# Holding side work behind later instructions in the attention stages of a hybrid decoder step

## The chip, the cores and the metric

The kernel runs on one core of one Trainium2 chip. A core has a matrix engine (TensorE, PE in the profile, with its weight loads as PEld), a vector engine (VectorE, DVE), an activation engine (ScalarE, ACT), a general engine (GpSimd, POOL) and a queue engine (SyncE, SP) that issues most of the transfers. The metric is the device time of one execution in microseconds (us); lower is better. Each engine works through its own list of instructions, whose order is fixed when the kernel is built.

## The reference, cut to what matters

One inference step of a one-layer decoder trunk is computed, for a prompt of 512 tokens and for a sample group of eight sequences of eight new tokens, each with 2048 tokens in a paged cache. Two attention branches run beside each other: forgetting attention ("fox") and sparse attention ("nsa"), which has a compressed, a selected ("slc") and a window ("win") part. Prompt and sample share all weights. Cut to what the change touches:

```python
def fox_attend(q, cq, q_pos, k, v, ck, k_pos):
    s = jnp.einsum('btgrd,bsgd->bgrts', q, k).astype(jnp.float32) * HEAD_DIM ** -0.5
    bias = jnp.moveaxis(cq, 1, -1)[..., :, None] - jnp.moveaxis(ck, 1, -1)[..., None, :]
    p = masked_softmax(s + bias, k_pos[None, :] <= q_pos[:, None])
    return jnp.einsum('bgrts,bsgd->btgrd', p.astype(v.dtype), v)

# in nsa_attend: which 16 of the blocks of 64 keys a query reads
imp = block_importance(jnp.sum(p_c, axis=2), n_sel)          # from the compressed scores
score = jnp.where(blk <= cur, imp + jnp.where(forced, FORCE_BONUS, 0.0), -jnp.inf)
_, idx = lax.top_k(score, min(N_SELECT, n_sel))
```

## The kernel before, in words

The change touches two stages.

**Prompt attention** (about 290 to 443 us of the trace). Its loop `for n, (br, r) in enumerate(steps + [(None, None)])` takes twelve steps: slc0, slc1, win0, win1, slc2, slc3, win2, win3, fox0 to fox3. A step scores two heads (g = 0, 1) in four query tiles each: two or three matmuls into one of four PSUM banks ("mm"), one vector instruction that adds the bias, writes the scores to SBUF and leaves their extreme (`tensor_tensor_reduce`, line 1253; `Swin`, `Sfox` in the profile; its instruction is kept as `last_min`), and one exponential on ACT (kept as `last_soft`). In the same step the step before is finished: its weights are turned over on PE (`ptwin`, `ptfox`), copied to SBUF by ACT and, one in three, by DVE (`turn_over`; `PTwin`, `PTfox`), multiplied with the values into a bank of a second pair ("acc"; `owin`, `ofox`), and scaled on DVE (`Wwin`, `oT`). Between these lie pieces of the conditioning projection (`adat`, `ada`, `adw`, `modT`).

Three steps also build the queries of later steps: `qstack` is called at n = 2 (nsa, second half), n = 6 (fox, first half, read from fox0 on) and n = 8 (fox, second half). It turns four tiles over into an "acc" bank for each of two heads, and for each of two halves of that bank ACT writes the rounded queries (line 1216) and DVE the rest (`stt`, line 1217, an instruction by `scalar_tensor_tensor` at line 110; `qstnsa`, `qstfox`). So one stack is four `stt` on DVE, each after an ACT instruction, and the ACT instruction of a bank's second half after the `stt` of its first.

The sample group's selection of blocks is computed beside this, as side work: `sample_cmp` at n = 2 (softmax of the compressed scores), `sample_importance` at n = 3, `sample_compare` at n = 6 (three pairwise comparisons of 30 x 30), `sample_rank` at n = 7 (two sums over them, lines 1446 and 1447, and four small ones), `sample_select` at n = 8 (tables and the turned selection). Most of it is DVE work; it writes tiles of a scratch that the profile calls `Dt`, and `rank`.

**Sample attention** (from 443 us). The loop over s = 0 to 15 takes a pair of sequences n = s // 4 and a quarter i = s % 4 of their cache: `key_rows` turns key rows over (`k`) and copies them (`kt`, by ACT and by DVE), `pair_scores` scores (`ss`) and takes the extreme on DVE (line 1794, `sS`) and the exponential on ACT, `turn_weights` turns over (`sp`, copied to `spT`), `values` multiplies (`so`). Rows come from HBM through the SP queue, a few quarters ahead. Beside it, `forget_split` cuts a sequence's sums of log forget values in three bf16 parts (`DH`, with `DR` as scratch: two ACT and two DVE instructions), for the sequences 0 and 1 ahead of the loop and for later pairs in the steps s = 1, 5, 9. `sample_maps` builds the tables that sort the summed rows (`maps`: one GpSimd instruction and fifteen DVE ones), ahead of the loop; the first `sums`, after s = 4, read them.

**What sets the order.** The program lists its instructions in the order of writing; a planner then puts each engine's instructions in an order of its own, by when its inputs are ready in its plan and, among those that are ready, the one written first. `issue_after(x)` holds every instruction of its block that runs on the engine of x behind x, and does nothing to the other engines' ones. The side work is held behind `last_min`, the last `tensor_tensor_reduce` of its step.

Of the kernel before, what the change touches and what calls it, by code (L numbers as in the profile page):

```python
# [6 lines left out]
F32 = mybir.dt.float32  # L7
# [3 lines left out]
AF = mybir.ActivationFunctionType  # L11
OP = mybir.AluOpType
# [16 lines left out]
LOW = -3.0e38  # L29
# [17 lines left out]
class Step:  # L47
# [1002 lines left out]
    def prompt_attention(self, pk, pn, pp):  # L1050
# [22 lines left out]
        for n, (br, r) in enumerate(steps + [(None, None)]):  # L1073
# [64 lines left out]
            side = {2: self.sample_cmp, 3: self.sample_importance, 6: lambda: self.sample_compare(pn), 7: self.sample_rank,  # L1138
                    8: self.sample_select}
            if n in side:  # L1140
                with self.tc.issue_after(self.last_min):
                    side[n]()
            if n == 11:
                with self.tc.issue_after(self.last_min):
# [60 lines left out]
    def qstack(self, pp, which, c0, gi, rp, gs=(0, 1)):  # L1205

        st = {}
        for g in gs:
            tb = self.stackb(f"q{which}{rp}{g}")
            for i in range(4):  # L1210
                self.tr(tb[:, P * i:P * i + P], self.zc(c0 + 64 * (4 * g + 2 * rp), P)[:, i])
            for e in range(2):
                lo = slice(64 * e, 64 * e + 64)
                hi = slice(64 - 64 * e, 128 - 64 * e)
                s = pp.tile([P, SEQ], F32R, tag="qst", bufs=4, name=f"qst{which}{rp}{g}{e}")
                self.act(s[lo], tb[lo], scale=self.gcol[lo, gi:gi + 1])
                self.stt(s[hi], tb[lo], self.gcol[lo, gi:gi + 1], s[lo].bitcast(F32), OP.mult, OP.subtract)
                st[g, e] = s
        return st

# [409 lines left out]
    def sample_attention(self, sp, sp0):  # L1630
        nc = self.nc
        self.E = self.op2.tile([P, 4, 64], BF16, name="E")
        self.tt(self.E, self.tok[:, 0:4, None].to_broadcast([P, 4, 64]), self.hot[:, None, :].to_broadcast([P, 4, 64]), OP.mult)
        self.chain = ""
        self.wk, self.S, self.DT, self.T, self.stat = {}, {}, {}, {}, {}
        self.sob = [self.accb(f"so{x}") for x in range(2)]
        self.keys, self.DH = {}, {}
        self.rooms(sp)
        for o in range(2):
            self.key_rows(sp, 0, o)  # L1640
            self.forget_split(sp, o)
            self.forget_turned(sp, o)
        for b in range(2):
            self.window_load(sp, b)
        for u in range(6, 11):
            self.sample_load(sp, u)
        self.sample_maps(sp)
        ns = 2 * NB
        for s in range(ns + 1):
            n, i, on = s // 4, s % 4, s < ns  # L1650
            if on:
                if i == 2:
                    for o in range(2):
                        self.window_keys(sp, 2 * n + o)
                self.pair_scores(sp, s)
                if i == 2:
                    self.window_scores(sp, n)
                    self.window_weights(n)
                if i == 1:
                    for o in range(2):  # L1660
                        if n < 3:
                            self.forget_split(sp, 2 * n + 2 + o)
            if s + 1 < ns:
                self.key_rows(sp, s + 1, 0)
            if on and i == 3:
                self.window_turned(sp, n)
            for g in range(2):
                if s:
                    self.values(s - 1, g)
            if s and i == 0:  # L1670
                self.pair_end(sp, n - 1)
            if s + 1 < ns:
                self.key_rows(sp, s + 1, 1)
            if i == 3 and n < 3:
                for o in range(2):
                    self.forget_turned(sp, 2 * n + 2 + o)
            if s == ns - 4:

                self.hH = self.keep.tile([P, NK, NT], F32R, tag="r2", bufs=1, name="hH")
                late = self.small.tile([P, 1], F32, tag="late", bufs=1, name="late")  # L1680
                with self.tc.issue_after(nc.gpsimd.tensor_copy(late, self.keys[0, 0][:, 0:1]).ins):
                    self.dma("gpsimd", self.hH, self.hfd[:, :, 0:NT])
            if on:
                for g in range(2):
                    self.turn_weights(sp, s, g)
            if s == ns:
                self.g0 = self.mix_first(self.w0, self.mmb, 0)
            if s == ns or n and i == 1:
                self.sums(n - 1)
            if on and i == 3:  # L1690
                self.window_values(sp, n)
                self.window_end(sp, n)
                for o in range(2):
                    if n < 3:
                        self.window_load(sp, 2 * n + 2 + o)
            for u in (2 * s + 9, 2 * s + 10):
                if s and u < 4 * NB:
                    self.sample_load(sp, u)
            if s == ns - 2:

                sp0.close()
                self.mix_open()
# [67 lines left out]
    def pair_scores(self, sp, s):  # L1770

        n, i = s // 4, s % 4
        bs = 2 * n, 2 * n + 1
        bd = self.bdF, self.bdN
        pbs = [self.mmb(f"ss{s}{g}") for g in range(2)]
# [14 lines left out]
        nm, dn = self.stat[n]  # L1790
        S = self.S[s] = [sp.tile([P, 576], F32, tag=f"S{2 * (s % 2) + g}", bufs=1, name=f"sS{s}{g}") for g in range(2)]
        ttr, w = self.nc.vector.tensor_tensor_reduce, 512
        for g in range(2):
            ttr(S[g][:, 0:512], pbs[g], self.ramp[g], -1.0, -LOW, OP.add, OP.min, nm[:, i, g:g + 1])
        if i == 3:
            w = 576
            pn = self.mmb(f"sn{n}")
# [7 lines left out]
                    own[:, g:g + 1])  # L1805
            self.tt(nm[:, 3], nm[:, 3], own, OP.min)
        for g in range(2):
            self.act(S[g][:, 0:w], S[g][:, 0:w], AF.Exp, bias=nm[:, i, g:g + 1], scale=-1.0, accum_out=dn[:, i, g:g + 1])

    def turn_weights(self, sp, s, g):  # L1810
        S = self.S[s][g]
# [883 lines left out]
```

## Time and profile before

| | us |
|---|---|
| median of 3 runs (1158.37 to 1158.73) | 1158.49 |
| the profiled execution's own time | 1155.07 |
| its span | 1153.4 |
| PE busy | 1131.6 (98% of the span) |
| DVE busy | 801.5 (69%) |
| ACT busy | 581.0 (50%) |
| POOL busy | 275.7 (24%) |

Times inside the trace are counted in us from the start of the span. The profiled execution ran 3.42 us under the median of the runs, and its span is 1.67 us shorter than its own time. Busy time says how long an engine had an instruction in work; matmuls overlap, so PE at 98% is not PE at its best rate. The granted clock of TensorE was 1.0 throughout.

### The profile page before, as it was taken

To read this page: it belongs to the slowest core of one execution; us is meant where nothing else is said; L and a number is where in the kernel's file an instruction comes from. 1 tells how busy PE (TensorE), PEld (TensorE's weight loads), DVE (VectorE), ACT (ScalarE), POOL (GpSimd) and SP (SyncE) were. 2 spreads that over 40 slices of the span, in tenths; PEclk is the share of its full clock that TensorE was granted. 3 is DMA by queue.
4 is the path that set the end of the run, shared out by engine and by line. 5 is a ranking of instruction groups with operands and counts; after the bars stand their busy time and mean duration, and the time that the engine had idled before them with its cause. 6 is when DMAs were issued, how large, how long until landed. Compare 5 with 4: busy or idle time off the path is not lost.

```text
span 1153.4 us, 25215 instructions
## 1 busy us (share of the span) xinstructions
PE 1131.6 (98%) x9434; PEld 966.6 (84%) x9434; DVE 801.5 (69%) x1937; ACT 581.0 (50%) x1151; POOL 275.7 (24%) x337
## 2 busy tenths in 40 slices
PE   8999999999999999999999999999999999999998
PEld 5888789999766565777899999789999998888887
DVE  4688785687776895776655454667867744798686
ACT  3455463444776785565532223447565655565420
POOL 4302100000220120001678670010656411110100
PEclk9999999999999999999999999999999999999999
DMA  9997456797684669999999994447444637877732
GB/s 221 229 263 222 151 152 200 242 319 237 191 257 160 209 213 317 293 317 328 233 287 301 330 289 159 119 132 223 148 149 147 188 113 255 318 257 252 240 119 83
DMA packets 188188, 255.51 MB, mean 222 GB/s; under 512 B 23161, under 2 KB 144706, under 8 KB 185890
## 3 DMA queue, kind: packets, MB, share of 16 engines
q1 hardware_dynamic: 148770, 173.03, 48.8%
q0 software_dynamic: 21296, 67.38, 18.2%
q10 hardware_dynamic: 18000, 13.50, 4.0%
q8 instruction: 74, 1.21, 0.4%
q14 instruction: 48, 0.39, 0.1%
HBM read 217.64 MB, written 57.12 MB: 238 GB/s over the span
## 4 chain that ended last, share of the span: by engine, by line
PE 82%; DVE 8%; issue 3%; DMA 3%; ACT 2%; POOL 1%; SPq 0%; POOLq 0%; ACTq 0%; DVEq 0%
PE dn L78 14%; PE z L78 9%; PE mg L78 8%; PE hid L78 5%; PE br L78 4%; PE wo L78 4%; PE up L78 3%; PE k L84 2%; PE ct L84 2%; PE ada L78 2%; PE dns L78 2%; PE ss L78 2%; PE so L78 1%; PE oslc L78 1%; PE sp L84 1%
## 5 line engine op out<-in xcount | busy, mean ns | idle before, releaser
L78 PE MATMUL z<-winh,h 128*128 128x264 f32 (+1 forms) x576 | 110.9, 286 | 0.3
L78 PEld LDWEIGHTS z<-winh,h 128*128 128x128 f32 x576 | 91.7, 190 | 2.1 <-DVE h L808 0.9
L78 PE MATMUL z<-winl,h 128*128 128x264 f32 (+1 forms) x320 | 88.1, 284 | 0.0
L113 ACT ACTIVATE xh<-ct 128x256 fp32r<-128x256 f32 x128 | 48.0, 385 | 58.3 <-PE ct L84 30.4
L78 PE MATMUL mg<-hH,wmh 128*128 128x288 f32 x240 | 70.8, 297 | 1.3 <-ACT mgt L113 1.3
L78 PE MATMUL mg<-hH,wml 128*128 128x288 f32 x240 | 70.5, 296 | 0.0
L78 PE MATMUL mg<-hL,wmh 128*128 128x288 f32 x240 | 68.4, 295 | 0.0
L132 DVE TENSOR_TENSOR xl<-ct,xh 128x256 fp32r<-128x256 f32 x128 | 51.8, 421 | 13.3 <-ACT xh L113 11.4
L78 PEld LDWEIGHTS z<-winl,h 128*128 128x128 f32 x320 | 60.6, 190 | 0.0
L132 DVE TENSOR_TENSOR wml<-wmr,wmh 128x1024 fp32r<-128x1024 f32 x14 | 19.2, 1371 | 43.3 <-ACT wmh L113 43.3
L78 PEld LDWEIGHTS mg<-hH,wmh 128*128 128x128 f32 x240 | 45.2, 188 | 1.6 <-ACT mgt L113 1.5
L78 PEld LDWEIGHTS mg<-hH,wml 128*128 128x128 f32 x240 | 45.2, 188 | 0.0
L132 DVE TENSOR_TENSOR wp<-sums,wp 128x1024 fp32r<-128x1024 f32 x26 | 39.0, 1510 | 8.5 <-ACT wp L113 7.9
L78 PE MATMUL hid<-xh,w1hlv 128*128 128x512 f32 (+1 forms) x160 | 43.9, 361 | 0.5 <-ACT xh L113 0.4
L78 PEld LDWEIGHTS mg<-hL,wmh 128*128 128x128 f32 x240 | 44.3, 188 | 0.0
L78 PE MATMUL hid<-xh,w1hlk 128*128 128x512 f32 (+1 forms) x160 | 44.0, 361 | 0.1
L132 DVE TENSOR_TENSOR wp<-pu,wp 128x512 fp32r<-128x512 f32 (+1 forms) x26 | 30.7, 1187 | 17.9 <-ACT wp L113 17.8
L113 ACT ACTIVATE mgt<-mg 128x288 f32<-128x288 f32 x32 | 12.8, 410 | 56.3 <-PE mg L78 56.2
L2060 POOL TENSOR_TENSOR td<-td 128x512 f32<-128x512 f32 x24 | 34.0, 1416 | 18.9 <-DMA td<-in_w_down 18.5
L84 PE MATMUL k<-identF,rows 128*128 128x128 f32 x256 | 35.6, 280 | 2.8 <-ACT kt L113 1.5
L78 PE MATMUL br<-oL,wbh 128*128 128x288 f32 x128 | 37.7, 295 | 0.0
L78 PE MATMUL br<-oH,wbl 128*128 128x288 f32 x128 | 37.7, 294 | 0.0
(1178 smaller groups left out, 3640.0 us busy)
## 6 DMA issues: line engine op xcount, KB each, us to landing
adw<-in_w_ada SPq DMA_DIRECT2D x16, 1024.0 KB
foxD<-in_cache_fox_kv SPq DMA_DIRECT2D x128, 128.0 KB
rows<-in_cache_nsa_kv SPq DMA_DIRECT2D x128, 128.0 KB
rows<-foxD SPq DMA_DIRECT2D x26, 512.0 KB
pu<-in_w_up SPq DMA_DIRECT2D x26, 512.0 KB
wdr<-in_w_down SPq DMA_DIRECT2D x26, 512.0 KB
cpg<-in_cache_nsa_kv SPq DMA_DIRECT2D x96, 128.0 KB
td<-in_w_down POOLq DMA_DIRECT2D x24, 512.0 KB, 6.1
```

Of the source, the lines that this page charges most:

```text
L78: ins = self.nc.tensor.matmul(out, a, b, start=start, stop=stop, skip_group_check=True)
L84: ins = self.nc.tensor.transpose(out, in_, self.identF[:n, :n])
L113: return self.nc.scalar.activation(out, in_, f, **kw)
L132: self.splits.append((eng or self.nc.vector).tensor_tensor(l, x, h.bitcast(F32), op=OP.subtract).ins)
L2060: self.nc.gpsimd.tensor_tensor(out, x, y, op=OP.subtract)
```

## The change

It has two parts. In prompt attention, the side work at n = 2, 3, 6, 7 and 8 is held behind `last_stack` as well as behind `last_min`; `last_stack` is the last `stt` of the latest `qstack`. So the DVE instructions of n = 2 and 3 come behind the fourth `qstnsa` instruction, those of n = 6 and 7 behind the fourth `qstfox` instruction of the first half, and those of n = 8 behind the fourth of the second half.

In sample attention, `forget_split` in the steps s = 1, 5, 9 is held behind that step's last extreme on DVE (`last_low`) and its last exponential on ACT (`last_exp`), and `sample_maps` moves from ahead of the loop to s = 1, behind the same two. No instruction is added or removed.

```diff
-                with self.tc.issue_after(self.last_min):
+                with self.tc.issue_after(self.last_min), self.tc.issue_after(self.last_stack):
                     side[n]()
...
-                self.stt(s[hi], tb[lo], self.gcol[lo, gi:gi + 1], s[lo].bitcast(F32), OP.mult, OP.subtract)
+                self.last_stack = self.stt(s[hi], tb[lo], self.gcol[lo, gi:gi + 1], s[lo].bitcast(F32), OP.mult, OP.subtract)
...
         for u in range(6, 11):
             self.sample_load(sp, u)
-        self.sample_maps(sp)
...
                 if i == 1:
-                    for o in range(2):
-                        if n < 3:
-                            self.forget_split(sp, 2 * n + 2 + o)
+                    with self.tc.issue_after(self.last_low), self.tc.issue_after(self.last_exp):
+                        for o in range(2):
+                            if n < 3:
+                                self.forget_split(sp, 2 * n + 2 + o)
+                        if n == 0:
+                            self.sample_maps(sp)
...
-            ttr(S[g][:, 0:512], pbs[g], self.ramp[g], -1.0, -LOW, OP.add, OP.min, nm[:, i, g:g + 1])
+            self.last_low = ttr(S[g][:, 0:512], pbs[g], self.ramp[g], -1.0, -LOW, OP.add, OP.min, nm[:, i, g:g + 1]).ins
...
-            self.act(S[g][:, 0:w], S[g][:, 0:w], AF.Exp, bias=nm[:, i, g:g + 1], scale=-1.0, accum_out=dn[:, i, g:g + 1])
+            self.last_exp = self.act(S[g][:, 0:w], S[g][:, 0:w], AF.Exp, bias=nm[:, i, g:g + 1], scale=-1.0,
+                                     accum_out=dn[:, i, g:g + 1]).ins
```

## The prediction

> **What bounds the kernel now.** I read the page first, for the span and the engines' shares.
>
> ```profile
> span 1153.4 us, 25215 instructions
> PE 1131.6 (98%) x9434; PEld 966.6 (84%) x9434; DVE 801.5 (69%) x1937; ACT 581.0 (50%) x1151; POOL 275.7 (24%) x337
> PE 82%; DVE 8%; issue 3%; DMA 3%; ACT 2%; POOL 1%; SPq 0%; POOLq 0%; ACTq 0%; DVEq 0%
> ```
>
> PE is the bound as a whole, and 82% of the chain that ended last. An edit that only reorders DVE work can gain or lose nothing but PE's idle time, and only in the two stages where it acts. Next, the busy time per engine in stretches of these stages (stretch, length, then PE, PEld, DVE, ACT, POOL, the granted clock, DMA share, GB/s).
>
> ```profile
> 327.00:345.00 18.00, 17.39 (x138) 11.61 (x137) 17.07 (x58) 14.72 (x42) 3.60 (x3) 1.00 0.79 255
> 384.40:397.00 12.60, 10.93 (x90) 7.47 (x88) 12.22 (x34) 9.92 (x26) 0.61 (x1) 1.00 0.72 229
> 399.90:404.00 4.10, 4.10 (x40) 2.44 (x39) 2.09 (x5) 2.89 (x5) 0.92 (x2) 1.00 0.66 183
> 404.00:432.00 28.00, 26.71 (x190) 18.43 (x188) 27.47 (x108) 23.16 (x65) 8.34 (x17) 1.00 0.70 213
> 446.00:452.50 6.50, 5.42 (x69) 3.44 (x70) 5.75 (x18) 3.15 (x10) 0.00 (x0) 1.00 0.96 315
> ```
>
> Here DVE is as full as PE: 17.07 of 18.00, 12.22 of 12.60, 27.47 of 28.00. Only at 399.9 to 404.0 has it room (2.09 of 4.10). So in these stages DVE sets the end as often as PE, and where on its queue a piece of side work lies is worth as much as the piece is long. Third, the chain of waits from 384 to 400 (start, us, what), with two rows of PE's timeline behind it that show what the chain's end holds up.
>
> ```profile
> 386.67 0.86 DVE Dt L1446
> ...
> 387.59 1.70 DVE Dt L1447
> ...
> 389.36 0.76 DVE qstfox L110
> ...
> 391.19 0.69 ACT qstfox L113
> ...
> 396.37 0.61 DVE PTwin L116
> ```
>
> ```profile
> 390.17 2.37 PE L78 MATMUL owin<-PTwin,zN 128*64 128x512 f32 x16 [1.53 <-DVE qstfox L110]
> 397.03 0.44 PE L84 MATMUL ptwin<-identF,Swin 128*128 128x128 f32 x2 [0.16 <-DVE PTwin L116]
> ```
>
> The two sums of `sample_rank` (lines 1446, 1447) lie on the path, ahead of the second of the four `qstfox`. PE waits 1.53 us for that: the bank that `owin` wants is the one the stack is still read from. At 397.03 PE waits for DVE again, 0.16 us, so this whole run of DVE work decides where PE stands there.
>
> **Part one, the side work of the prompt.** Where does held work go when its pin has run? In DVE's timeline of before it starts in the same 10 ns (start, us, engine, line, operation, tiles):
>
> ```profile
> 372.86 0.68 DVE L1253 CUSTOM_DVE_ANT_0 Swin<-swin,brownsa 128x512 f32<-128x512 f32 x1
> ...
> 373.47 2.10 DVE L101 TENSOR_TENSOR rank<-Dt 128x900 bf16<-128x900 f32 x2
> 375.48 0.68 DVE L101 TENSOR_TENSOR klfox<-ktfox,khfox 64x512 fp32r<-64x512 f32 x1
> ...
> 376.66 1.00 DVE L101 TENSOR_TENSOR rank<-rank 128x900 bf16<-128x900 bf16 x1
> ...
> 386.58 1.08 DVE L1446 TENSOR_REDUCE Dt<-rank 128x30 f32<-128x900 bf16 x1
> ...
> 398.53 0.61 DVE L105 TENSOR_SCALAR Dt<-Dt,prow 128x256 f32<-128x256 f32 x2
> ...
> 399.53 0.22 DVE L101 TENSOR_TENSOR Dt<-triU,Dt 64x64 f32<-64x64 f32 x1
> 399.90 0.20 DVE L1261 RECIPROCAL denfox<-denfox 128x8 f32<-128x8 f32 x1 [0.15 <-ACT Sfox L113]
> ```
>
> The comparisons start at 373.47 behind the extremes of win2, the sums at 386.58 behind those of win3, the tables of `sample_select` at 398.53 behind those of fox0. Something else slips in only between links of the side work's own chain (375.48 to 376.66). I take it that after the change each piece starts right behind the last `stt` of its stack.
>
> *n = 6 and 7.* Taking the sums out from ahead of the second `qstfox` removes 0.86 + 1.70 = 2.56 us from the chain. PE gets back its 1.53 us, and with the 0.16 at 397.03 at most 1.69. The stack then ends at 389.6 at the earliest: 386.67 + two `stt` of 0.76, the ACT instruction of 0.69 that waits for the second of them, and the last `stt` of 0.76. But behind it come now the sums, 1.08 + 1.70 = 2.8, and the three comparisons too, 2.10 + 1.00 = 3.1, which until now ran at 373 to 377 behind a full PE. Queued behind them on DVE are the extremes of fox0, `Wwin`, `oT` and `PTwin`; PE waits for these at 397.03, and for each extreme that frees a score bank. From 386.67 to the end of `PTwin` at 396.37 + 0.61 = 396.98 the chain is 10.31 us long and stays on DVE and on ACT behind DVE, so what goes ahead of `PTwin` lengthens it by its own duration. If all the sums and comparisons go ahead of `PTwin`, it ends 3.1 us later: a loss of 3.1, the upper end. If all goes behind it, PE gains 1.69, the lower end. If the longer sum (1.70), or as much of other links, slips behind, the loss is 3.1 - 1.7 = 1.4. The rows above show a start in the same 10 ns and slips of a microsecond between links, so I take **+1.4**. What is late next is PE's in-order work from 397 on, fox1 and the second stack with it; up to 404 nothing gives it back, since PE has 4.10 of 4.10 there.
>
> *n = 8.* The six small tables take 399.75 - 398.53 = 1.2 us, now just ahead of DVE's only room here. They go behind the last `stt` of the second stack:
>
> ```profile
> 410.36 0.75 DVE L110 SCALAR_TENSOR_TENSOR qstfox<-qfox,gcol,qstfox 64x512 fp32r<-64x512 f32 x1
> ...
> 431.71 0.55 PE L84 MATMUL ptfox<-identF,Sfox 128*128 128x128 f32 x3 [0.81 <-DVE PTfox L116]
> ```
>
> That is in the stretch with 27.47 of 28.00. PE idles 28.00 - 26.71 = 1.29 there, 0.81 of it at 431.71 on DVE. At most the tables add their 1.2 there, at least nothing. Only the stalls that name DVE would grow by all of it; PE is bound by itself between them, so I take **+0.4**. The turned selection (`selx`) and its copy follow a dozen us later, and the sample's scores want them only after 446.
>
> *n = 2 and 3.* The one long instruction that moves, and what it moves behind:
>
> ```profile
> 337.27 0.68 DVE L101 TENSOR_TENSOR Dt<-csc,Dt 128x508 f32<-128x508 f32 x1
> ...
> 339.13 0.76 DVE L110 SCALAR_TENSOR_TENSOR qstnsa<-qnsa,gcol,qstnsa 64x512 fp32r<-64x512 f32 x1
> ```
>
> ```profile
> 346.31 0.71 PE L84 MATMUL cpt<-identF,Dt 128*127 128x128 f32 x4 [0.50 <-DVE Dt L101]
> ```
>
> On a full DVE the `stt` comes 0.6 earlier, and the reduction of `Dt` that comes right behind it now starts about 0.5 later, as the moved instruction lies between them. PE waits for this chain at 346.31. Between 0 and +0.5; two extremes of `Sslc` can change places with it, so **+0.2**.
>
> **Part two, the start of sample attention.** The chain of waits, and the two timelines behind it:
>
> ```profile
> 447.18 0.20 DVE DH L101
> ...
> 447.52 1.20 DVE maps L107 x5
> 448.72 0.20 DVE DR L101
> 448.92 0.60 DVE sS L1794
> ...
> 450.14 0.21 DVE DH L101
> 450.34 0.61 DVE kt L116
> ...
> 456.16 1.02 PE k L84 x8
> ```
>
> ```profile
> 454.59 0.69 DVE L1794 CUSTOM_DVE_ANT_0 sS<-ss,scr 128x512 f32<-128x512 f32 x1
> ...
> 455.20 0.69 DVE L116 COPY kt<-k 128x512 f32<-128x512 f32 x1
> 457.22 0.69 DVE L116 COPY kt<-k 128x512 f32<-128x512 f32 x1 [1.33 <-PE k L84]
> ...
> 460.48 0.69 DVE L1794 CUSTOM_DVE_ANT_0 sS<-ss,scr 128x512 f32<-128x512 f32 x1 [1.98 <-PE ss L78]
> ...
> 482.08 1.06 PE L84 MATMUL k<-identF,rows 128*128 128x128 f32 x8 [0.71 <-DMA rows<-in_cache_nsa_kv]
> ```
>
> The tables (1.20) and two pieces of `forget_split` (0.20, 0.21) lie on the path to `kt` at 450.34, and PE is idle 6.50 - 5.42 = 1.08 in that stretch. The first extreme also waits for PE's scores, so it can come some 0.7 earlier, `kt` some 0.8: a gain up to 0.8. Against it: behind the extreme that ends at 455.20 wait the tables and the split: five tables at 1.20, a sixth of the same kind and nine small ones, some 2.0 us by estimate. The `kt` now at 455.20 can be queued behind them. It ends at 455.9, and half-way through the next eight turns of keys (456.16 + 0.5, about 456.6) PE wants its bank. If the tables go first PE loses 2.0 - 0.7 = 1.3; the idle 1.33 and 1.98 behind it hide them otherwise. In s = 5 and 9 nothing on PE's path follows. The row load that ends at 482.08 can take back part of either. Between -0.8 and +1.3, and by the row of the chain nearer to the gain: **-0.4**.
>
> **The sum:** +1.4 + 0.4 + 0.2 - 0.4 = +1.6 us. On the profiled execution: 1155.07 + 1.6 = 1156.7. It ran 3.42 under the median of the runs, so on that: 1158.49 + 1.6 = **1160.1**. About 0.2%, 2.3 us, is what a measurement can tell from no change, so this counts as the same: 1156.2 to 1160.8.
>
> **The rivals.** *One, the side work finds idle places.* The stall at 390.17 goes, the comparisons and sums fall in DVE's room at 399.9 to 404.0, the start of sample attention gains in full: -1.69 - 0.8 = -2.5, 1156.0. For it: no instruction wants the comparisons or the ranks before `sample_select`, which is a step later. Against: that room is 2.0 us and the work is 5.9, and pieces start with their pin.
>
> *Two, a new wait ahead of the weights of win3.* All 5.9 us run right behind the fourth `stt`; fox0's extremes wait, PE stops when its four score banks are full, and `PTwin` ends at 400.1. With all of the tables on the full stretch and `Dt` late: +3.1 + 1.2 + 0.5 = +4.8, 1163.3. It is slower as soon as over 2.3 us of DVE work net come between the stack and `PTwin`. For it: the 10 ns starts. Against: the slips between links. The Trainium skill, in "Perfetto Trace Analysis", section "Optimizing Scalar/DVE Operations", speaks for this rival: where DVE is saturated it advises fewer and larger operations, or another engine, and names no gain from order. The 12.22 of 12.60 agrees that DVE is saturated here. By that rule nothing is won at 390.17 but the place of the stall.
>
> *Three, it does nothing that can be seen:* what is won or lost before 482.08 is taken back by the row loads (share of DMA 0.96 at 446 to 452.5) and by PE's own slack: 1158.5. For it: 0.71 us of wait there. Against: the loads are issued behind PE's own progress, so they move with it.
>
> **How the numbers follow.** The forecast 0.40, of which 0.27 within 0.2% and 0.13 slower by more. Rival one 0.22: 0.17 faster, 0.05 within. Rival two 0.20, slower. Rival three 0.18: 0.13 within, 0.03 faster, 0.02 slower. Together 0.20 faster, 0.45 the same, 0.35 slower. The forecast's own range is 1158.5 to 1162.0; that for 8 in 10 reaches to both rivals, 1155.8 to 1163.0.
>
> **What would show it.** Right: no wait of 1.53 at `owin`; the sums and comparisons at about 390 to 396, and a new PE wait of 1 to 3 us for `Sfox` or `PTwin` before 400; DVE without the six tables before 399.9, and longer waits for `PTfox` near 432; `sS` of s = 0 at about 448.2 and the tables behind 454. Wrong: the comparisons in DVE's room after 399.9, or a PE without idle from 388 to 400 (rival one), or a `kt` of s = 2 that PE waits for.

## The result, and the profile after

The changed kernel takes 1166.9 us (median of six executions, 1164.95 to 1168.44) where the kernel before takes 1157.4 (median of seven, beside it on the same chip). The ratio is 1.0087, with a 95% interval of 1.0071 to 1.0103: some 10 us slower. The forecast was 1160.1, with 1155.8 to 1163.0 as its range, so it missed, and the time is longer than that of the slowest rival too (1163.3).

The execution that was profiled with this result ran its matmuls at about half the rate throughout (2355 us; its median `z` matmul took 538 ns, against 283 in the kernel before) and is left out, so the profile after that is read here is of another execution of the same kernel, 1169.65 us, called `e1_both` below. From its page: the span, the engines, and the engines' shares of the chain that ended last.

```profile
span 1168.0 us, 25208 instructions
PE 1139.0 (98%) x9434; PEld 969.9 (83%) x9434; DVE 800.8 (69%) x1937; ACT 580.4 (50%) x1151; POOL 275.8 (24%) x337
PE 87%; DVE 5%; DMA 4%; ACT 2%; issue 1%; SPq 0%; ACTq 0%; DVEq 0%
```

The work is the same: 9434 matmuls, 1937 DVE instructions, DVE busy 800.8 against 801.5. The span is 14.6 us longer, and PE, which does the same matmuls, counts 7.4 us more of busy time (1139.0 against 1131.6): in places they ran slower. The same stretches as before (stretch, length, then PE, PEld, DVE, ACT, POOL, granted clock, DMA share, GB/s):

```profile
384.40:397.00 12.60, 12.40 (x100) 8.65 (x98) 11.78 (x33) 11.21 (x33) 0.61 (x1) 1.00 0.78 236
399.90:404.00 4.10, 4.10 (x27) 2.54 (x27) 3.80 (x11) 2.46 (x7) 0.61 (x1) 1.00 0.35 108
404.00:432.00 28.00, 21.50 (x141) 14.73 (x142) 25.40 (x99) 20.11 (x54) 8.09 (x17) 0.93 0.30 80
```

Up to 404 the edit does what it was made for: PE's idle time in the first stretch falls from 1.67 to 0.20 us, and the new wait that the forecast had before 400 does not come. The loss is in the third row. PE's busy time falls from 26.71 to 21.50 of 28 us and its matmuls from 190 to 141, and the share of DMA from 0.70 to 0.30. Something that should have been loaded by then was not. PE's waits in that stretch (start, length, instruction, in brackets the idle time before it and who ended it):

```profile
410.87 0.38 PE L78 MATMUL sfox<-khfox,qstfox 128*128 128x256 f32 x1 [1.17 <-DVE nmfox L1253]
...
414.08 1.04 PE L78 MATMUL selx<-Dt 128*32 128x512 f32 x2 [0.55 <-DVE Dt L105]
...
428.83 0.47 PE L78 MATMUL sfox<-khfox,qstfox 128*128 128x128 f32 x1 [2.44 <-DVE nmfox L1253]
```

The last is a wait of 2.44 us for the score extremes (`nmfox`) of the head fox3. The chain of waits says what those waited for:

```profile
418.83 0.33 SPq L163
...
423.98 4.36 DMA browfox<-cumD
428.47 0.29 DVE Sfox L1253
428.83 2.37 PE sfox L78 x9
```

It leads to SP's queue and to a load of fox3's bias rows, `browfox`. SP's own rows, first of the kernel before and then of the changed one (start, time over which the group was issued, what):

```profile
408.04 3.93 SPq L163 DMA_DIRECT2D Dt<-lfD  x8
412.07 0.85 SPq L163 DMA_DIRECT2D browfox<-cumD  x2
...
414.18 0.32 SPq L163 DMA_DIRECT2D rows<-foxD  x1
```

```profile
418.83 5.10 SPq L163 DMA_DIRECT2D Dt<-lfD  x8
423.98 0.90 SPq L163 DMA_DIRECT2D browfox<-cumD  x2
...
425.54 0.53 SPq L163 DMA_DIRECT2D rows<-foxD  x1
```

`forget_load` brings the log forget values into `Dt`. The tables of `sample_select` are carved out of the same `Dt`, so this load has to wait until their last reader is done. SP works its list in order: behind the load stand the bias rows of fox3 and the whole row stream of sample attention. All of it is issued 11 to 12 us later. The waits of SP's queue between 395 and 430 say it in one line each, before and after (waited for: total, times, longest):

```profile
SPq L163 <- PE selx L78: 8.4, 1, 8.4
```

```profile
SPq L163 <- DVE Dt L101: 20.4, 1, 20.4
```

This wait was there before, 8.4 us long, and no wait of PE followed from it in that stretch. The forecast gave it no price. That is the start of the explanation, but the runs show that it is only half of one.

### The profile page after: what moved, and what is told of

It is laid out like the page before. It is cut to its first block, busy times and chain, and to the rows that moved or that the text cites. A ratio compares the mean times of both kernels' runs of the same rounds, so it can differ in the third digit from the quotient of the medians.

```text
span 2353.5 us, 25208 instructions
## 1 busy us (share of the span) xinstructions
PE 2344.9 (100%) x9434; PEld 1814.0 (77%) x9434; DVE 814.2 (35%) x1937; ACT 587.0 (25%) x1151; POOL 268.1 (11%) x337
## 4 chain that ended last, share of the span: by engine, by line
PE 99%; DVE 0%; issue 0%; ACT 0%; DVEq 0%; ACTq 0%
PE dn L78 14%; PE z L78 11%; PE hid L78 10%; PE mg L78 8%; PE wo L78 4%; PE br L78 4%; PE ct L84 3%; PE up L78 3%; PE k L84 3%; PE ada L78 2%; PE ss L78 2%; PE dns L78 2%; PE so L78 2%; PE sp L84 1%; PE idle L78 1%; PE sfox L78 1%
## 5 line engine op out<-in xcount | busy, mean ns | idle before, releaser
L78 PE MATMUL z<-winh,h 128*128 128x264 f32 (+1 forms) x576 | 242.7, 527 | 0.0
L78 PEld LDWEIGHTS z<-winh,h 128*128 128x128 f32 x576 | 205.5, 408 | 3.7 <-issue 2.7
L78 PE MATMUL z<-winl,h 128*128 128x264 f32 (+1 forms) x320 | 167.2, 524 | 0.0
L78 PEld LDWEIGHTS z<-winl,h 128*128 128x128 f32 x320 | 131.9, 412 | 0.1
L78 PE MATMUL hid<-xh,w1hlv 128*128 128x512 f32 (+1 forms) x160 | 98.7, 733 | 0.0
L78 PE MATMUL hid<-xh,w1hlk 128*128 128x512 f32 (+1 forms) x160 | 98.7, 733 | 0.0
L84 PE MATMUL ct<-identF,ro 128*128 128x128 f32 x256 | 83.7, 535 | 0.0
L78 PEld LDWEIGHTS hid<-xh,w1hlk 128*128 128x128 f32 x160 | 56.8, 377 | 19.3 <-issue 15.6
L78 PEld LDWEIGHTS hid<-xh,w1hlv 128*128 128x128 f32 x160 | 56.8, 383 | 18.6 <-issue 13.8
L78 PE MATMUL br<-oH,wbh 128*128 128x288 f32 x128 | 60.0, 468 | 0.0
```

The lines of the kernel that those rows point to most:

```text
L78: ins = self.nc.tensor.matmul(out, a, b, start=start, stop=stop, skip_group_check=True)
L84: ins = self.nc.tensor.transpose(out, in_, self.identF[:n, :n])
```

## The experiments

Ratios are to runs of the kernel before made beside it on the same chip, with 95% intervals; a cost in us is the ratio less 1, times the median of those runs. The expectations are as they were recorded; each says what its theories are. Theories D, E and F follow one another, as each of the first two fell.

### Which part costs

`e1_both` is the changed kernel itself. `e2_pins_prompt` has its part in prompt attention alone, the pins:

```diff
-                with self.tc.issue_after(self.last_min):
+                with self.tc.issue_after(self.last_min), self.tc.issue_after(self.last_stack):
```

`e3_sample_only` has its part in sample attention alone:

```diff
-        self.sample_maps(sp)
...
+                    with self.tc.issue_after(self.last_low), self.tc.issue_after(self.last_exp):
```

> The changed kernel as it is, for an undisturbed trace of it. Its runs stood 0.87% (some 10 us) above the kernel before, where the prediction had +1.6 us. Theory A (the pins in prompt attention cost it: the comparisons and sums come ahead of fox0's work, and everything planned behind them is placed anew): +8 to +10 us, with the loss between 384 and 450 us of the trace. Theory B (the moved tables and split sums in sample attention cost it): the loss lies behind 443 us. Theory C (a lower granted clock, since some of its runs showed 0.994 to 0.998): the loss is spread over the whole span in proportion to PE's work, and a run at 1.000 shows little of it.

> Only the pins in prompt attention (all of n = 2, 3, 6, 7, 8 behind the last stack); sample attention as before. Theory A: +8 to +10 us, all or nearly all of the whole change. Theory B: within 2 us of the kernel before, as the prediction had it (+2.0). Theory C: as before, or slower with a clock under 1.

> Only the second part: split sums and tables behind the step's extremes in sample attention; prompt attention as before. Theory A and the prediction's own term: -0.8 to +0.3 us. Theory B: +6 to +10 us.

| | ratio | interval |
|---|---|---|
| `e1_both` | 1.0086 | 1.0052 to 1.0120 |
| `e2_pins_prompt` | 1.0069 | 1.0043 to 1.0094 |
| `e3_sample_only` | 0.9981 | 0.9960 to 1.0003 |

The loss comes with the pins of prompt attention, within the intervals all of it. The part in sample attention costs nothing that can be seen; 0.0019 of 1159.8 is a gain of 2.2 us, and the interval just reaches no change.

### Which pin

`e4_pins_6_7` and `e5_pin_8` have the second pin at n = 6 and 7 alone and at n = 8 alone; `e8_only_7` is the changed kernel with it at n = 7 alone, `e7_without_8` the changed kernel without it at n = 8.

```diff
-                with self.tc.issue_after(self.last_min):
+                with self.tc.issue_after(self.last_min), self.tc.issue_after(self.last_stack if n in (8,) else self.last_min):
```

> Only the comparisons (n = 6) and the sums (n = 7) held behind the fourth query stack as well; n = 2, 3, 8 and sample attention as before. If these two carry the loss (theory A1): +5 to +9 us. If the tables of n = 8 carry it (theory A2, they now start behind the second fox stack, in a stretch where DVE is full): 0 to +2 us here. The prediction's term for this piece alone was +1.4 us.

> The kernel before with one pin added: only the tables of sample_select (n = 8) held behind the fourth stt of the second fox stack as well. Theory D (the queue): the DMA that loads the log forget values into the scratch Dt must wait for the last reader of sample_select's tables there; the SP queue stands still behind it (20.4 us in the changed kernel, 8.4 before), and with it fox3's bias rows and the stream of cache rows. Then the load's issue moves from 408 to 414 or later, the first row load from 414 to 420 or later, and the time rises by 4 to 8 us. Theory A (DVE work ahead of PE, the prediction's kind of term): +0.4 to +1.2 us, whatever SP does.

> The changed kernel without the pin at n = 8 (n = 2, 3, 6, 7 and sample attention as changed). By theory D the ranks still come some 8 us later than before, so the tables and the load of Dt are 2 us late and not 11: -1 to +2 us. If the pin at n = 8 is not what carries the loss: +5 us or more.

> The changed kernel with the added pin at n = 7 alone: the two sums behind the fourth stt, the comparisons left where they were at 373 us, n = 2, 3, 8 as before, sample attention as changed. If the stall of 1.53 us at 390 is worth what the chain showed, and the SP queue is not moved by over 2 us: -1 to -3 us. If the sums only push fox0's work by their own length: 0 to +2 us.

The traces do not run in step: at the first extreme of win0, ahead of every pin, they lie between 313.38 and 316.18. So the last column counts from that extreme to the first matmul of the sample's scores (`ss`) and says how much longer this is than the 131.42 us of the kernel before, in one execution of each. The two rows of before:

```profile
314.58 0.28 DVE L1253 CUSTOM_DVE_ANT_0 Swin<-swin,brownsa 128x128 f32<-128x128 f32 x1
```

```profile
446.00 0.69 PE L78 MATMUL ss<-kt,bdF 64*32 64x512 f32 x4
```

| | ratio | interval | `Dt` load starts | sample's scores later |
|---|---|---|---|---|
| before | 1 | | 408.04 | 0 |
| `e4_pins_6_7` | 1.0006 | 0.9982 to 1.0030 | 410.03 | 3.9 |
| `e5_pin_8` | 1.0109 | 1.0071 to 1.0147 | 417.28 | 9.6 |
| `e7_without_8` | 1.0033 | 1.0014 to 1.0052 | 411.60 | 2.5 |
| `e8_only_7` | 0.9995 | 0.9971 to 1.0018 | 408.54 | -0.3 |

The pin at n = 8 alone is as slow as the whole change, or slower: 0.0109 of 1157.8 is 12.6 us (the medians, 1170.27 and 1157.84, differ by 12.4), and 9.6 us are there when sample attention starts. It holds six tables that take 1.2 us of DVE. The pins at n = 6 and 7 cost 0.7 us, with an interval from -2.1 to +3.5. Of the 3.9 us in the trace of `e4`, 3.4 by estimate are a granted clock of 0.50 between 414 and 420, which falls behind a PE wait of 1.35 us at 412.68. `e8` has no PE wait at `owin` any more and gains nothing that the interval shows. The parts do not add up: `e7_without_8` holds only parts that are cheap or good in `e3` and `e4`, and the pins at n = 2 and 3, which were not run alone, and is 3.8 us slower. Of the 2.5 us in its trace 0.2 come with n = 2 and 3, as is shown below. Behind that the trace has PE waiting 0.81, 1.02 and 1.66 us for rows of the cache between 553 and 559 and 2.38 at 594. This execution took 1169.08, 7 us over the median of `e7`, so the others need not have these waits, and why they come there is not settled.

### Is it the late load?

Theory D said so. `e6_load_behind_rows` (the changed kernel) and `e9_pin_8_load_moved` (before with the pin at n = 8) issue the load into `Dt` behind the first row loads, so that nothing that PE needs soon stands behind it.

```diff
-            if n == 8:
-                self.forget_load()
...
                 for u in range(5):
                     self.sample_load(None, u)
+                    if u == 1:
+                        self.forget_load()
```

> The changed kernel with one thing moved on SP: the eight loads into Dt stand behind fox3's bias rows and the first two row loads instead of ahead of them, so only they wait for sample_select. All else is the changed kernel. Theory D: the row stream starts at about 414 to 416 again instead of 425.5, the wait of 2.4 us at 428.8 for fox3's first extremes goes, the loss behind 485 us (some 5 us) goes, and 5 to 9 of the 10 us come back; what is left is 1 to 5 us. Theory A: the time stays within 2 us of the changed kernel (+8 to +10 us).

> The kernel before with the pin at n = 8 (12 us slower by itself) and the eight loads into Dt behind fox3's bias rows and the first two row loads on SP. What is left is what the six tables cost as DVE work, the prediction's own term. Theory D: the queue was all but that term, so 0 to +3 us are left, the wait of 3.4 us for nbf at 426.8 shrinks below 1 us. Theory A: +8 us or more are left, since the tables stand on DVE as late as in the pinned kernel.

`e6` came to 1.0034 (1.0016 to 1.0052), but `e9` only to 1.0064 (1.0038 to 1.0089): of 12.6 us there remained 7.4, where the theory had 0 to 3. In both, the bias rows were issued at 407, earlier than before. The chain of waits of `e9` shows a second way from the load to PE:

```profile
425.05 2.15 DMA Dt<-lfD
...
427.48 1.96 DVE fscr L711
429.43 0.20 DVE Sfox L1253
...
429.69 2.31 PE sfox L78 x12
```

`fscr` is the sum over `Dt` in `forget_sums`. On DVE's list it stands ahead of fox3's extremes, so when `Dt` is late, they are late too. In `e6` the sum fell behind them (it starts at 428.10, the extremes at 425.85).

So the next two take the tables out of `Dt` and leave the load where it was. `e12_pin_8_own_tables` is `e5` and `e13_both_own_tables` the changed kernel, each with the tables in the tile that held the comparisons.

```diff
+        self.wide = pn.tile([P, 1024], F32, tag="wide", name="rank")
...
+        self.sel = self.wide[:, 0:32]
...
-        self.cut = self.mark
+        self.scr, self.cut = self.wide, 32
```

> As the run with only n = 8 pinned (ratio 1.0109), but the tables of the selection and the flags they read lie in the tile that held the comparisons, not in Dt, so the load into Dt need not wait for them; every instruction stays, with the same length. Theory D (the tables cost by what they hold: Dt, its load, and all that stands behind that load on SP's list and, by the sum of line 711, on DVE's): the first load into Dt starts at 408 or before, not at 417.28; the bias rows of fox3 at 412 or before; no wait of PE over 1.5 us between 425 and 432; ratio 0.999 to 1.003, that is at most 3 us of the 12.4 are left. The rival (the tables cost by their place on a full DVE, and by the slower clock that a short wait of PE then brings): the load is early as well, but the ratio stays at 1.006 or over, as it did when the load was moved behind the rows.

> The changed kernel with the tables in the tile of the comparisons, as in the run beside it. Here the ranks come late too (their last small instructions at about 407), and they still read Dt. Theory D: the load into Dt starts at 408 to 410, not 418.83; the ratio falls from 1.0086 to 1.000 to 1.004, that is to that of the changed kernel without the pin at n = 8 (1.0033) or below. The rival (place on DVE): 1.006 to 1.009.

The load started at 399.27 and 404.74, the bias rows at 406.74 and 408.44. The ratios were 1.0073 (1.0050 to 1.0097) and 1.0080 (1.0058 to 1.0103). Theory D fell: with an early load most of the loss stays. DVE's rows of `e12` show what holds fox3's extremes now:

```profile
418.43 0.68 DVE L1253 CUSTOM_DVE_ANT_0 Sfox<-sfox,browfox 128x512 f32<-128x512 f32 x1
...
419.76 2.00 DVE L711 TENSOR_REDUCE fscr<-Dt 128x256 f32<-128x1024 f32 x1
...
426.53 0.29 DVE L1253 CUSTOM_DVE_ANT_0 Sfox<-sfox,browfox 128x128 f32<-128x128 f32 x1
```

From the extreme at 418.43 to the one at 426.53 DVE does almost nothing but side work. In the kernel before the longest stretch from one extreme to the next between 405 and 432 is 3.35 us:

```profile
420.60 0.69 DVE L1253 CUSTOM_DVE_ANT_0 Sfox<-sfox,browfox 128x512 f32<-128x512 f32 x1
...
421.21 1.98 DVE L711 TENSOR_REDUCE fscr<-Dt 128x256 f32<-128x1024 f32 x1
...
423.95 0.28 DVE L1253 CUSTOM_DVE_ANT_0 Sfox<-sfox,browfox 128x128 f32<-128x128 f32 x1
```

In every kernel with the pin at n = 8 up to here it was between 6.2 us (`e6`) and 10.3 (`e9`), in every kernel without it, those below included, between 2.8 (`e17`) and 4.5 (`e14`). With the tables at 411 to 414, where they stood at 398, their followers (`selx`, `cumn`, `ncnt` and their copies) fall in with the tables of `sample_tables` and with the sums. What used to lie between the extremes of fox2 is now one block behind them.

### Is it the block?

Theory E said so. `e15_pin_8_sums_later` and `e16_both_sums_later` are `e5` and the changed kernel with the sums a step later; `e17_before_sums_later` is the control.

```diff
             if n == 10:
-                self.forget_sums(pn)
                 self.sample_load(None, 5)
+            if n == 11:
+                self.forget_sums(pn)
```

> As the run with only n = 8 pinned (ratio 1.0109), with the sums of forget_sums taken a step later (n = 11, behind the extremes of fox3). The load into Dt stays late (417.28) and the rows of fox3 and the row stream stay behind it. Theory E (the lump): held tables bring selx, cumn, ncnt and all that follows them on DVE to the same place as the sums, so that DVE works 8 to 10 us between 418 and 428 with no extreme in it, and PE runs out of scores; without the sums the stretch with no extreme is under 6.5 us, PE's wait at 425 to 430 is under 1 us, and the ratio falls to 1.002 to 1.007. Theory D (the late load, by SP's list): the bias rows of fox3 come as late as they did (422.25), PE waits as long, and the ratio stays at 1.008 to 1.012.

> The changed kernel (ratio 1.0086) with the sums at n = 11. Theory E: stretch of DVE with no extreme 6 to 7 us instead of 9.39, no PE wait over 1.5 us at 428, no slow clock there; ratio 1.002 to 1.005, like the run in which the load was moved behind the rows (1.0034, 6.18 us), since there too the sums fell behind the extremes of fox3. Theory D: the load stays at 418.8 and fox3's bias rows at 424; ratio 1.006 to 1.010.

> Control: the kernel before with the sums at n = 11. Both theories: the stretches with no extreme are 3 to 4 us already, the load starts at 408; ratio 0.998 to 1.001.

The control is 1.0005 (0.9990 to 1.0020). `e15` is 1.0081 (1.0061 to 1.0101) and `e16` 1.0113 (1.0088 to 1.0138): no gain that the intervals show, and theory E fell as D had. DVE's rows of `e15` name the reason, with the load late as it had been:

```profile
426.81 0.29 DVE L1254 CUSTOM_DVE_ANT_0 Sfox<-sfox,browfox 128x128 f32<-128x128 f32 x1 [1.43 <-DMA browfox<-cumD]
```

The sums are out of the block, but now DVE stands idle for the bias rows. The extremes start at 426.81, and at 426.53 in `e12`. Each cause alone holds them to within 0.3 us of the same time.

### Both at once

Theory F: two causes side by side, of which the later decides. `e18_pin_8_both_cures` is `e5` with the edits of `e12` and `e15` together.

> As the run with only n = 8 pinned (ratio 1.0109), with both edits: the tables out of Dt, and the sums of forget_sums at n = 11. Theory F (two causes side by side, of which the later sets the start of fox3's extremes: with the load cured the block with the sums holds them until 426.53, with the sums cured the landing of their bias rows holds them until 426.81): the extremes of fox3 start at 424.5 to 425.7, no wait of PE over 1 us at 425 to 430, no slow clock there, and the ratio falls to 1.001 to 1.005, as in the changed kernel with the load behind the rows (425.85, 1.0034), the one run in which both were out of the way. Rival: most of the cost is older than 424, from the tables and their followers between 410 and 420, where all kernels with this pin have waits of 0.5 to 1.2; then the extremes may come earlier, but the ratio stays at 1.006 or over.

The ratio is 1.0025 (1.0001 to 1.0049). The one cure left 8.4 us (`e12`), the other 9.4 (`e15`), both left 2.9, of 12.6 (by the medians 9.8, 10.6 and 3.9 of 12.4). The interval with both cures ends at 1.0049, and those with one begin at 1.0050 and 1.0061. SP's and DVE's rows of `e18`:

```profile
398.40 6.08 SPq L163 DMA_DIRECT2D Dt<-lfD  x8
405.87 3.49 SPq L163 DMA_DIRECT2D browfox<-cumD  x2
```

```profile
423.90 0.29 DVE L1254 CUSTOM_DVE_ANT_0 Sfox<-sfox,browfox 128x128 f32<-128x128 f32 x1
...
428.68 1.98 DVE L711 TENSOR_REDUCE fscr<-Dt 128x256 f32<-128x1024 f32 x1
```

The extremes start at 423.90, earlier than the expectation had them and as they did before (423.95; `e18` was 1.2 us ahead until then, so it lost 1.2). The long wait of PE is gone, and the clock stays at 1.000. Over all kernels with the pin at n = 8:

| | bias rows issued | `fscr` sum | fox3's extremes | PE's longest wait, 420 to 432 | ratio | sample's scores later |
|---|---|---|---|---|---|---|
| before, without the pin | 412.07 | 421.21 | 423.95 | 0.81 | 1 | 0 |
| `e5` | 422.25 | 423.89 | 428.41 | 3.43 | 1.0109 | 9.6 |
| `e1` | 423.98 | 425.77 | 428.47 | 2.44 | 1.0086 | 10.0 |
| `e2` | 423.60 | 426.11 | 428.02 | 1.13 | 1.0069 | 6.6 |
| `e9` | 407.36 | 427.48 | 429.35 | 2.16 | 1.0064 | 8.9 |
| `e12` | 406.74 | 419.76 | 426.53 | 2.25 | 1.0073 | 7.5 |
| `e13` | 408.44 | 419.28 | 427.05 | 1.94 | 1.0080 | 7.0 |
| `e15` | 422.50 | 433.00 | 426.81 | 0.97 | 1.0081 | 6.5 |
| `e16` | 422.32 | 432.75 | 426.60 | 1.83 | 1.0113 | 7.4 |
| `e6` | 407.17 | 428.10 | 425.85 | 0.25 | 1.0034 | 3.7 |
| `e18` | 405.87 | 428.68 | 423.90 | 0.47 | 1.0025 | 3.4 |

The two in the last rows are the only ones with the bias rows early and the sum behind the extremes, and the only ones under 1.006. In their traces the sample's scores start 3.7 and 3.4 us later than before, in all others 6.5 to 10.0. Theory F holds. The intervals of `e6` and `e9` overlap, so it rests on `e18` and on the traces more than on the ratio of `e6`. The order within the upper group does not follow the start of the extremes, and with intervals of 0.004 to 0.008 it need not.

The traces of `e5`, `e12`, `e15` and `e18`, which differ in the cures alone, also say how the loss divides up to the sample's scores. A clock at half rate takes 3.4, 1.7, 1.7 and 0 us of it, by estimate from windows of 2 us; without that the scores start 6.2, 5.8, 4.8 and 3.4 us late. So of the 9.6 us of `e5` some 3.4 stay with both cures, 2.7 are the later of the two causes, and 3.4 the clock that fell in the wait that they brought. One kernel does not fit this: in `e2` 3.4 of the 6.6 us are a slow clock at 412 to 420, ahead of fox3's extremes, and without it `e2` would stand with `e18`.

Of what is left in `e18`, 2.0 us lie where its expectation's rival put the whole: PE's waits of 0.50, 0.73 and 0.81 between 410 and 415.5, two of them for DVE while the tables pass there and one for ACT. As far as these waits go, this is the place's own price.

### A better version

Side work can also be taken earlier. `e10_sums_early` has no pin on the stack and takes `sample_rank` at n = 6 right behind the comparisons; `e11_both_early` takes the comparisons at n = 5 and the ranks at n = 6. Both keep the part in sample attention. `e14_early_own_tables` is `e11` with the tables out of `Dt`.

```diff
-            side = {2: self.sample_cmp, 3: self.sample_importance, 6: lambda: self.sample_compare(pn), 7: self.sample_rank,
+            side = {2: self.sample_cmp, 3: self.sample_importance, 5: lambda: self.sample_compare(pn), 6: self.sample_rank,
```

> A candidate: no pin behind the query stacks; the two sums and the four small ones of sample_rank follow sample_compare at n = 6 (about 378 to 381 us, where DVE waited 0.4 to 0.5 us at a time for PE) instead of at n = 7, ahead of the stack; sample attention as changed. If the stall of 1.53 us at 390 goes and nothing on the SP queue becomes later: -1 to -3 us against before. If the sums delay win3's extremes by their 2.8 us: 0 to +2 us.

> A second candidate: sample_compare at n = 5 (about 362 to 372 us, where DVE was idle 1.5 + 0.9 + 0.3 us) and sample_rank at n = 6, each behind its step's extremes only; sample attention as changed. If DVE takes the comparisons in its idle time: -1 to -3 us, and the stall at 390 is gone. If they delay win2's extremes: 0 to +3 us.

> The kernel with the comparisons at n = 5 and the ranks at n = 6 (ratio 0.9972), with the tables in the tile of the comparisons. The load into Dt started at 405.15 there, behind the tables; now it can start once the ranks have been read, about 398. If the load's place is worth something beyond before's, the ratio falls to 0.994 to 0.997; if SP's rows are not what PE waits for once they are in time, it stays at 0.996 to 0.999; if an earlier load into Dt meets the row loads at 390 to 404 (share of DMA 0.72 and 0.66 there), it rises to 0.999 or over.

`e10` is 0.9991 (0.9965 to 1.0017), `e11` 0.9972 (0.9944 to 0.9999), `e14` 0.9991 (0.9971 to 1.0010). The stretch in which before PE waited 1.53 us is full in `e11`, and so is nearly all of the next (two rows of the windows, columns as above):

```profile
384.40:397.00 12.60, 12.60 (x98) 8.19 (x96) 11.51 (x39) 12.28 (x37) 0.61 (x1) 1.00 0.88 261
404.00:432.00 28.00, 26.47 (x182) 17.02 (x182) 26.45 (x109) 23.43 (x66) 6.58 (x8) 1.00 0.79 244
```

So the stall that the change went for can be had without its cost. In the traces of `e11` and `e14` the sample's scores start 2.0 and 2.2 us earlier than before, counted as above, and in `e3`, with the same part in sample attention, neither earlier nor later: the order alone is worth 2 us there, in one execution of each. Over the whole kernel the 3.2 us of `e11` stand only just clear of no change, and `e14` does not confirm them: an earlier load into `Dt` than 405 buys nothing that can be seen.

## Why the prediction was wrong

**What bounds the kernel.** Right: in these stretches DVE decides, and place on its queue is worth as much as length. But it stopped at DVE. The queue that loads into the work's scratch, SP's, was not priced.

**n = 6 and 7, forecast +1.4.** The number lies within what can be measured, +0.7 (-2.1 to +3.5) in `e4`, but the way to it was another one, so this was luck. The 1.53 us at `owin` are gone. The planner let a part slip behind `PTwin`, as I had taken it, though more than the longer sum (DVE's rows of the changed kernel):

```profile
392.13 0.76 DVE L110 SCALAR_TENSOR_TENSOR qstfox<-qfox,gcol,qstfox 64x512 fp32r<-64x512 f32 x1
392.90 2.10 DVE L101 TENSOR_TENSOR rank<-Dt 128x900 bf16<-128x900 f32 x2
...
398.46 0.68 DVE L116 COPY PTwin<-ptwin 128x512 f32<-128x512 f32 x1
399.06 0.22 DVE L317 TENSOR_REDUCE adw<-adat 128x18 f32<-128x72 f32 x1
399.20 1.08 DVE L1446 TENSOR_REDUCE Dt<-rank 128x30 f32<-128x900 bf16 x1
400.20 1.73 DVE L1447 TENSOR_REDUCE Dt<-rank 128x30 f32<-128x900 bf16 x1
```

Two comparisons run right behind the fourth `stt`, the third at 397.32, both sums behind `PTwin`. `PTwin` starts at 398.46, where it started at 396.29, so the chain on DVE became longer as forecast; but the new PE wait of 1 to 3 us before 400 that I named as a sign did not come (0.20 at 395.73 is all), because PE's list had `ada` and score tiles to do in the meantime (397.02, 398.02). Up to 404 PE gained some 1.5 us where the forecast had it lose 1.4. What I left out is the other end: the sums now end at 402, so in `e4` `selx` comes 2 us later (408.92, before 406.93), and PE waits 1.35 us at `cumn` (412.68) for its followers.

**n = 8, forecast +0.4.** This is the step that failed, and it failed by 12 us: `e5` measures +12.6 (8.2 to 17.0), and taking the pin out of the changed kernel gives back 0.53% of 1157.8, 6.1 us. The sentence that failed is that at most the tables add their 1.2 us there, and with it the last one, that `selx` and its copy "follow a dozen us later" to no harm. (In `e5` `selx` starts at 412.34, before at 406.93, and `cumn` at 418.01, before at 410.40.) I costed six instructions by their length and asked only who waits for their results. I did not ask who waits for the storage that they give back (`Dt`, its load, and all that SP does behind it), nor where their followers then fall (one block with the sums, ahead of fox3's extremes). Both lead to the same place, fox3's extremes, 2.8 to 5.3 us late in the runs with one cure or none, counted from the first extreme of win0. With both cures 2.9 us stay (0.1 to 5.7), so the 0.4 for DVE's own part is not refuted by the ratio; in the trace 3.4 are left. The wait of 8.4 us on SP's queue, which names `selx` as what ends it, was in the trace of before.

**n = 2 and 3, forecast +0.2.** Right up to where it was read: the wait at `cpt` grew by 0.24 us (before 0.50),

```profile
346.29 0.71 PE L84 MATMUL cpt<-identF,Dt 128*127 128x128 f32 x4 [0.74 <-DVE Dt L101]
```

and from the first extreme of win0 to these matmuls it is 31.92 to 31.95 us in the six kernels with these pins and 31.72 to 31.74 in the thirteen without: 0.2 us. What the two pins cost to the end of the kernel was not measured alone.

**Part two, forecast -0.4.** Right as far as it can be seen: `e3` gives -2.2 us, with -0.4 inside its interval. DVE's rows of `e3`:

```profile
447.44 0.69 DVE L1796 CUSTOM_DVE_ANT_0 sS<-ss,scr 128x512 f32<-128x512 f32 x1 [1.05 <-PE ss L78]
...
448.67 0.69 DVE L116 COPY kt<-k 128x512 f32<-128x512 f32 x1
...
454.05 0.15 DVE L105 TENSOR_SCALAR maps<-prow 128x1 f32<-128x1 f32 x1
```

The first extreme comes at 447.44 (448.83 before), `kt` at 448.67 (450.26 before), and the tables start behind 454. The trace of `e3` is 0.77 us ahead of the one of before from win0 on, so the change gains 0.6 us at the extreme and 0.8 at `kt`, where 0.7 and 0.8 were forecast. At the extremes of the second quarter (452.82, before 453.97) 0.4 us of it are left. The tables are sixteen DVE instructions, ten of them small, one more than the count beforehand. The price against it, `kt` queued behind the tables, did not come: the planner put that copy between them, at 454.30.

**The rivals.** One (idle places) was wrong on the sign, though its signs came up to 404: PE almost without idle time from 388 to 400, and the sums in DVE's room (399.20 to 401.93). Two had the right sign and the wrong place: its new wait was to come ahead of win3's weights, and that did not come. Three was refuted.

**The rest of the loss.** In `e1` the sample's scores start 10.0 us later than before, of the 14.6 us between the spans (1153.4 and 1168.0). The rest is met with in sample attention: waits for rows of 0.79, 1.64 and 0.22 us between 561 and 564, and the clock at half rate behind them until 568, some 1.7 us by estimate. Why rows come late there in some of the traces (`e1`, `e7`) and not in others (`e5`, `e6`) is open; the start of the row stream (425.5 in `e1`, 417.5 in `e7`, 423.8 in `e5`, 415.6 in `e6`) does not sort them.

## What to carry to other kernels

When work is moved later, price what it gives back as well as what it computes: find who is to overwrite its scratch, on which in-order queue that load stands, and what stands behind it. A wait on a queue that costs nothing today is the slack that the move spends. And where a cure brings nothing, look again at what the late instruction waits for now: with two causes that end at the same time, each cure alone can look useless.

## What the runs showed of the hardware

The granted clock falls after short waits. In `e1`, windows of 2 us around the wait for fox3's extremes (columns as above; the clock is the third number from the end):

```profile
426.00:428.00 2.00, 0.39 (x4) 0.15 (x2) 1.73 (x1) 0.00 (x0) 1.55 (x1) 1.00 0.96 111
428.00:430.00 2.00, 1.17 (x6) 1.08 (x7) 1.53 (x7) 1.13 (x4) 0.00 (x0) 0.53 1.07 278
430.00:432.00 2.00, 2.00 (x9) 1.36 (x9) 1.20 (x6) 1.60 (x7) 0.00 (x0) 0.50 0.93 362
432.00:434.00 2.00, 2.00 (x3) 0.39 (x3) 1.14 (x7) 1.89 (x7) 0.00 (x0) 0.50 1.07 401
434.00:436.00 2.00, 2.00 (x10) 1.02 (x10) 0.71 (x3) 0.20 (x1) 0.00 (x0) 0.77 1.07 350
```

Some 7 us at half clock cost some 3.4 us, an estimate from these rows (what each lacks to 1.00, times 2 us), on top of the wait. So a wait has a second price. Over the nineteen traces of these experiments and of the kernel before, between 25 and 1145 us: in or behind all 8 PE waits of 2.7 us and more (2.73 to 4.75) the clock fell, for 3 to 7 us; with 10 of the 28 waits of 1.5 to 2.5 us it fell too, and with 18 it did not, 2.45 (`e13`, 589) among them. Shorter ones were enough at times: 0.39, 0.25 and 0.97 us between 424 and 427 in `e15`, 1.17 and 0.50 at 411 to 412 in `e2`, 1.35 at 412.68 in `e4`. The same waits left it at 1.00 elsewhere, 1.17 and 0.50 in `e1` (410.87, 411.94) and 1.35 in `e7` (414.26), so the length of a wait alone does not decide. The clock is not the bulk of the loss: over the executions of `e1` its mean is 0.9956, against 0.9983 in those of before beside it, which makes some 3 of 10 us by estimate; one execution of the changed kernel with the clock at 1.000 on the mean took 1164.95, still 7.5 us over before, and `e13`, whose profile shows no drop, has a span of 1163.5, against 1153.4 of before.

The Trainium skill, in "TensorE: Matmul & The Clock Gate", section "HAM oscillation — how this bites in real kernels", gives as the rule to leave no idle gaps of PE over about 3.4 us. The half rate agrees (0.50 here); as a threshold the figure does not, since the clock fell at each of the eight waits from 2.73 us on, and once at one of 1.35. The section behind it, "A second HAM failure mode: psum-queue depth-cycling", tells of an oscillation from frequent short idle times of PE, and the short waits close together in `e15` agree with that.
